# Scan products in pairs of runs, projections in a written order, and a new order of the first products, in a hybrid encoder layer

## The chip, the cores and the metric

The kernel runs on one core of one Trainium2 chip. Its metric is the device time of one execution in microseconds (us). Of an execution with the profiler there is a trace as well; its span runs from the first to the last instruction of the core.

## The reference

One layer works on 288 tokens: 256 of a new stream (prompt) and 32 of a running one (sample). Everything is float32.

```
xn   = rmsnorm(x);  proj = xn @ w_in          -> u (1024), z (2048), xBC (2560), dt (32)
pool = (mean over the last 2/4/8/16 tokens of u, minus u) @ w_pool, scaled
xs, B, C = silu(causal conv of 4 over xBC);   dt = softplus(dt + bias)
y    = exact chunked scan of xs with dt, B, C and a state h0, plus D * xs       (32 heads of 64)
ssd  = grouped rmsnorm(y * silu(z))
x    = x + rmsnorm(concat[pool, ssd] @ w_out)
x    = x + rmsnorm((silu(gate) * value) @ w_down),  gate, value = conv of 3 over rmsnorm(x) @ w_up
```

The outputs are x for both groups of tokens and the new histories and states. `w_in` is 2048 x 5664, `w_out` 3072 x 2048, `w_up` 2048 x 11264, `w_down` 5632 x 2048.

## The kernel before, in words

**Products.** Channels lie on the 128 partitions and the 288 tokens along the free axis. A float32 factor is split into a high and a low part (fp32r), and a product of two tiles is three matmuls of 128x128 by 128x288 (`mm3`, L150 to L156): high weight by high activation, high by low, low by high. All three go to one PSUM accumulator. Where a part of a group is *turned* (`TURNED`, counted by group and part), the last two change places.

**Groups.** `project` makes one or more blocks of 256 output columns. It fetches weights on SP's queue (`fetch_w`), splits them with ACT (high part, L146) and DVE (low part, L147) in parts of 4 input tiles by 256 columns, four buffers each, and issues 24 matmuls a part. A group on `w_in` has four parts, 96 matmuls. In the order of the program, groups 1 to 8 make xs, 9 to 16 make z, 17 to 19 make u, 20 to 25 use `w_out`, and from 26 on `w_up` and `w_down` follow. Tiles of PSUM: five for accumulators, three ("aux") for the rest.

**The first products.** Before group 1, B, C, the last two tiles of u, and dt are made from `w_first` in 11 chunks of 1, later 2, input tiles (`CHUNKS`; matmuls L379, those of dt L386). Six blocks of 128 columns come from each chunk. Chunk 0 arrives as three pieces: blocks 2 and 3, blocks 4 and 5, blocks 0 and 1. High and low weights of a chunk lie in one tile `w`, `W_GAP` floats apart. Twelve matmuls on ones (L284, tile `busy`) run before the first data are there. These products are issued in a written order.

**The scan.** The 32 heads are taken in eight runs of four (`ssd_quad`, q = 0 to 7), two 128-channel tiles of xs each. A run needs g broadcast to all partitions (`gb`, L597, POOL's queue), xs with tokens on partitions (`xk`, L611, POOL's queue), and then:

- xk times its weights on DVE (L628)
- the mask m, 128 x 4 x 416: twelve ACT operations (L633), one exponential on ACT (L636), one product on DVE (L638); m has two buffers
- 16 matmuls of 64 output channels, eight for each of the two tiles, two at a time on the two halves of the array's columns: k = 0, 1 the prompt (L651, L653), k = 2, 3 the sample (L655, L657). Each is two instructions in the trace; a run has 32
- two additions to xs on DVE, straight from PSUM

`XS_RATE` and `Z_RATE` say after which group of xs or z a run stands in the program. Gating with z, squares and their sums follow; two sums over channels (`psum_t`, L710) stand at the end of the sixth z group and of group 17.

**What sets the order on TensorE.** A scheduler orders each engine's instructions at build time by a modelled timeline: an instruction goes when its inputs are ready in the model, the earliest of the program first. `tc.issue_after(ins)` puts what it encloses behind `ins` on the same engine; `tc.keep_in_program_order(ins)`, called `pin`, puts an instruction behind the one that the program wrote last on its engine. Products in `project` are not pinned before; all but the first of a run's products are.

**w_out.** Groups 20 to 25 take input tiles 8 to 15, 16 to 23 (both ssd), then 0 to 7 (pool). Group 20 has two blocks of 256 columns, groups 21 to 24 one, group 25 two. Pool groups 1 and 0 (12 matmuls each, `pool_group`) are written into group 20, ahead of the splits of tiles 16 to 23.

## Time and profile before

| What | Before |
|---|---|
| median of 3 runs, us | 1308.37 |
| the runs, us | 1307.97 to 1308.87 |
| the profiled execution's own time, us | 1308.33 |
| its span, us | 1306.6 |
| TensorE instructions | 10043 |
| DVE, share of the span | 68% |
| ACT, share of the span | 51% |
| granted TensorE clock, mean | 0.999 |

The profiled execution's time is 1.7 us above its span; what the span shows is what the kernel's order decides. Starts and durations in rows are in us from the span's start. A row of the timeline gives start, duration from the first start to the last end, engine, line, operation, tiles, shapes, and count; in brackets stands the engine's idle time before it and what ended it. A row of the chain gives start, time, engine and tile, line, and count: there, time over count is the distance from one matmul's start to the next one's, which is the rate of TensorE. A matmul's own duration (294 ns for 128x288) overlaps its neighbours' and is no rate.

### The profile page before, as it was taken

To read this page: it belongs to the slowest core of one execution; us is meant where nothing else is said; L and a number is where in the kernel's file an instruction comes from. 1 tells how busy PE (TensorE), PEld (TensorE's weight loads), DVE (VectorE), ACT (ScalarE), POOL (GpSimd) and SP (SyncE) were. 2 spreads that over 40 slices of the span, in tenths; PEclk is the share of its full clock that TensorE was granted. 3 is DMA by queue.
4 is the path that set the end of the run, shared out by engine and by line. 5 is a ranking of instruction groups with operands and counts; after the bars stand their busy time and mean duration, and the time that the engine had idled before them with its cause. 6 is when DMAs were issued, how large, how long until landed. Compare 5 with 4: busy or idle time off the path is not lost.

```text
span 1306.6 us, 25261 instructions
## 1 busy us (share of the span) xinstructions
PE 1299.5 (99%) x10043; PEld 1289.3 (99%) x10043; DVE 894.7 (68%) x1515; ACT 672.8 (51%) x1013; POOL 244.8 (19%) x399
## 2 busy tenths in 40 slices
PE   9999999999999999999999999999999999999998
PEld 9999999999999999999999999999999999999997
DVE  7999988879645588977766643345666666754454
ACT  7557767446544566544444433334444444444442
POOL 2342212222222221211211100001111111201110
PEclk9999999999999999999999999999999999999999
DMA  9568875445666468766554445455544554466653
GB/s 345 187 212 278 292 218 182 162 153 201 213 218 212 154 198 259 214 186 190 174 171 162 157 174 171 158 180 174 182 162 162 175 174 169 162 233 188 212 180 115
DMA packets 110038, 251.75 MB, mean 193 GB/s; under 512 B 64736, under 2 KB 73856, under 8 KB 87392
## 3 DMA queue, kind: packets, MB, share of 16 engines
q1 hardware_dynamic: 103568, 233.36, 54.7%
q0 software_dynamic: 5824, 16.13, 4.1%
q8 instruction: 78, 1.28, 0.4%
q10 hardware_dynamic: 528, 0.66, 0.2%
q14 instruction: 40, 0.33, 0.1%
HBM read 237.11 MB, written 13.00 MB: 191 GB/s over the span
## 4 chain that ended last, share of the span: by engine, by line
PE 98%; DVE 0%; DMA 0%; ACT 0%; ACTq 0%; issue 0%
PE acc L156 91%; PE acc L379 2%; PE acc_x L156 1%; PE acc_x L379 1%; PE py L651 1%; PE acc L1283 0%; PE acc L1284 0%; PE py L653 0%; DMA raw<-in_w_first 0%; PE acc_t L1306 0%; PE pst L992 0%; PE acc L386 0%; DVE rm L1046 0%; PE py L657 0%; PE py L655 0%
## 5 line engine op out<-in xcount | busy, mean ns | idle before, releaser
L147 DVE TENSOR_TENSOR wlo<-raw,whi 128x1024 fp32r<-128x1024 f32 (+1 forms) x396 | 473.0, 1196 | 303.3 <-ACT whi L146 302.3
L146 ACT ACTIVATE whi<-raw 128x1024 fp32r<-128x1024 f32 (+1 forms) x396 | 408.2, 1032 | 466.6 <-PE acc L156 375.6
L156 PE MATMUL acc<-hn,whi 128*128 128x288 f32 x2752 | 538.6, 294 | 0.4 <-ACT hn L1059 0.4
L156 PEld LDWEIGHTS acc<-hn,whi 128*128 128x128 f32 x2752 | 436.4, 188 | 1.0 <-ACT hn L1059 0.9
L156 PE MATMUL acc<-hn,wlo 128*128 128x288 f32 x1376 | 399.7, 291 | 0.0
L156 PEld LDWEIGHTS acc<-hn,wlo 128*128 128x128 f32 x1376 | 258.9, 188 | 0.0
L156 PE MATMUL acc<-fa,whi 128*128 128x288 f32 x1320 | 257.5, 293 | 0.0
L156 PE MATMUL acc<-xn,whi 128*128 128x288 f32 x1216 | 239.1, 294 | 0.0
L156 PEld LDWEIGHTS acc<-fa,whi 128*128 128x128 f32 x1320 | 208.9, 188 | 0.0
L156 PEld LDWEIGHTS acc<-xn,whi 128*128 128x128 f32 x1216 | 193.1, 188 | 0.7 <-issue 0.5
L156 PE MATMUL acc<-fa,wlo 128*128 128x288 f32 x660 | 192.1, 291 | 0.0
L156 PE MATMUL acc<-xn,wlo 128*128 128x288 f32 x608 | 177.6, 293 | 0.0
L156 PEld LDWEIGHTS acc<-fa,wlo 128*128 128x128 f32 x660 | 124.3, 188 | 0.0
L1109 POOL COPY fc_stage<-ebuf 128x4 f32<-128x4 f32 x88 | 26.4, 299 | 471.6 <-DVE ebuf L1108 450.7
L156 PEld LDWEIGHTS acc<-xn,wlo 128*128 128x128 f32 x608 | 114.4, 188 | 0.1
L156 PE MATMUL acc<-mixs,whi 128*128 128x288 f32 x512 | 100.5, 294 | 0.0
L1115 DVE SCALAR_TENSOR_TENSOR fc<-ebuf,cols,fc 128x290 f32<-128x290 f32 x176 | 90.4, 517 | 3.9 <-ACT fc L1113 1.1
L1113 ACT ACTIVATE fc<-ebuf,cols 128x290 f32<-128x290 f32 x88 | 54.4, 623 | 73.2 <-DVE ebuf L1108 71.1
L1104 POOL COPY ebuf<-cols 128x2 f32<-128x2 f32 x88 | 69.9, 794 | 108.4 <-DVE fc L1115 96.0
L156 PEld LDWEIGHTS acc<-mixs,whi 128*128 128x128 f32 x512 | 81.3, 188 | 0.0
L156 PE MATMUL acc<-mixs,wlo 128*128 128x288 f32 x256 | 74.1, 293 | 0.0
L156 PE MATMUL acc<-mixp,whi 128*128 128x288 f32 x256 | 50.2, 293 | 0.0
(322 smaller groups left out, 1241.0 us busy)
## 6 DMA issues: line engine op xcount, KB each, us to landing
raw<-in_w_up SPq DMA_DIRECT2D x80, 1024.0 KB, 5.1
raw<-in_w_in SPq DMA_DIRECT2D x38, 1024.0 KB, 5.2
raw<-in_w_down SPq DMA_DIRECT2D x32, 1024.0 KB, 4.9
raw<-in_w_out SPq DMA_DIRECT2D x24, 1024.0 KB, 5.1
raw<-in_w_down SPq DMA_DIRECT2D x16, 768.0 KB, 4.2
raw<-in_w_up SPq DMA_DIRECT2D x14, 512.0 KB, 4.4
gb<-g_d POOLq DMA_DIRECT2D x8, 832.0 KB, 5.8
raw<-in_w_first SPq DMA_DIRECT2D x5, 768.0 KB, 12.3
```

What stands on the lines that cost most here:

```text
L146: act.activation(hi, raw[:, k : k + n, :], AF.Copy)
L147: dve.tensor_tensor(lo, raw[:, k : k + n, :], hi.bitcast(F32), op=ALU.subtract)
L156: pe.matmul(out, w, a[:, x, :], start=start and n == 0, stop=stop and n == 2)
L379: pin(pe.matmul(first[m], w[r][:, k, m * P : (m + 1) * P], xn[kb + k][:, x, :], start=kb + k + r + x == 0, stop=kb + k == KD - 1 and r == 1,))
L651: ins = pe.matmul(y[c, 0:256], xw[:, 0, f_], m[:, h, 0:256], start=True, stop=False)
L1104: pool.tensor_copy(e[:, 258:260], hist_f[:, :, i])
L1109: pool.tensor_copy(fc_stage[:, :, :, i], e[:, 256:324].rearrange("p (s c) -> p s c", c=34)[:, :, 0:2])
L1113: act.activation(c, e[:, 0:290], AF.Identity, bias=col["f_b"][:, i : i + 1], scale=f_w[:, 0, i : i + 1])
L1115: dve.scalar_tensor_tensor(c, e[:, r_ : r_ + 290], f_w[:, r_, i : i + 1], c, op0=ALU.mult, op1=ALU.add)
```

## The change

Four edits go together.

- **Runs in pairs.** `ssd_quad` is cut into the masks (`ssd_masks`) and the products (`ssd_products`). Masks are made for one run after a group as before (XS 2, 4, 7 and z 0, 2, 3, 4, 5); the products of two runs stand together after XS group 7 and z groups 1, 4 and 6, numbered from 0, so at the end of groups 8, 10, 13 and 15. A run's twelve ACT operations are queued behind the exponential of the run before. The prompt columns of a run's two tiles share one PSUM tile, and the sample columns of the pair share another, so an addition to xs becomes two (256 and 32 columns).
- **Program order.** From group 6 to 19 every product is pinned. In groups 20 and 21 the low weight comes first, and the other two of the three matmuls are pinned behind it. The list of turned parts is another, and can name several parts of a group.
- **First products.** In chunk 0, blocks 2 and 3 get all three of their matmuls first, then blocks 4 and 5, then 0 and 1. Chunks 4 and 5 take low-weight products second. High and low weights lie 48 floats apart instead of 16; `sq2` is 16 floats longer; `busy` takes the buffer of `sq`, and `ones_r`, made earlier, replaces it in the sums of squares.
- **Pool products later.** Pool groups 1 and 0 are written between the two column blocks of tiles 16 to 23 in group 20, whose last eight tiles are taken as 4 to 7, then 0 to 3.

```diff
@@ -37,8 +37,10 @@
 MW = 416
 EVAC = 100
 SUMS_AFTER = 2
-XS_RATE = (0, 0, 1, 0, 1, 0, 1, 0)
-Z_RATE = (1, 0, 1, 1, 0, 1, 1, 0)
+XS_RATE = (0, 0, 1, 0, 1, 0, 0, 1)
+Z_RATE = (1, 0, 1, 1, 1, 1, 0, 0)
+PAIR_XS = (7,)
+PAIR_Z = (1, 4, 6)
 TAIL = NT - P
 NB = 768
 CHUNKS = ((0, 1), (1, 1), (2, 1), (3, 1), (4, 1), (5, 1), (6, 2), (8, 2), (10, 2), (12, 2), (14, 2))
@@ -53,10 +55,14 @@
 TURN_AT = 13
 FC_GAP = 48
 NEAR = 8
-W_GAP = 16
-W_ROOM = 32
+W_GAP = 48
+W_ROOM = 64
+TURNED_FIRST = (4, 5)
+WHOLE = (20, 21)
+FIRST_WHOLE = 6
 TURNED = {
-    1: 0, 5: 3, 7: 2, 8: 1, 10: 1, 12: 1, 13: 1, 15: 1, 16: 1, 18: 1, 20: 8, 22: 0, 27: 0, 28: 1, 46: 0, 65: 0,
+    1: (0,), 5: (3,), 9: (0,), 11: (0,), 14: (0,), 15: (0,), 16: (0,), 18: (0,), 20: (0,), 22: (0,), 27: (0,),
+    28: (1,), 46: (0,), 65: (0,),
 }
 
 
@@ -148,16 +154,22 @@
             out.append([(kb + k + i, hi[:, i, :], lo[:, i, :]) for i in range(n)])
         return out
 
+    whole = [False]
+
     def mm3(out, wh, wl, a, start, stop, other=False):
         pairs = [(wh, 0), (wh, 1), (wl, 0)]
+        if whole[0] == 2:
+            pairs = pairs[2:] + pairs[:2]
         if other:
             pairs[1:] = pairs[:0:-1]
         for n, (w, x) in enumerate(pairs):
-            pe.matmul(out, w, a[:, x, :], start=start and n == 0, stop=stop and n == 2)
+            ins = pe.matmul(out, w, a[:, x, :], start=start and n == 0, stop=stop and n == 2)
+            if whole[0] and (n or whole[0] == 1):
+                pin(ins)
 
     groups_done = [0]
 
-    def project(view, groups, acts, ksplit, before=None, done=None, spare=(), hold=(), behind=None, wait=(), tail=()):
+    def project(view, groups, acts, ksplit, before=None, done=None, spare=(), hold=(), behind=None, wait=(), tail=(), middle=None):
 
 
         n_all = sum(-(-w // P) for _, w in groups)
@@ -165,7 +177,8 @@
         accs.extend(spare)
         k_first, k_last = ksplit[0][0], ksplit[-1][0] + ksplit[-1][1] - 1
         groups_done[0] += 1
-        turned = TURNED.get(groups_done[0])
+        turned = TURNED.get(groups_done[0], ())
+        whole[0] = (FIRST_WHOLE <= groups_done[0] <= WHOLE[1]) + (groups_done[0] in WHOLE)
         n_part = 0
         after = before(*ksplit[0]) if before else None
         for i, (kb, n) in enumerate(ksplit):
@@ -174,7 +187,9 @@
             if before and i + 1 < len(ksplit):
                 nxt = before(*ksplit[i + 1])
             m0 = 0
-            for raw, (c0, w) in zip(raws, groups):
+            for r, (raw, (c0, w)) in enumerate(zip(raws, groups)):
+                if middle and (i, r) == (1, 1):
+                    middle()
                 parts = split_w(raw, kb, n, w, tuple(wait) + ((after or ()) if m0 else ()) + (hold if i else tail if m0 + w // P == n_all else ()))
                 for q, part in enumerate(parts):
                     for m in range(w // P):
@@ -183,7 +198,7 @@
                             if behind and part[-1][0] == k_last and m0 + m > SUMS_AFTER:
                                 order.enter_context(tc.issue_after(behind[-1].ins))
                             for k, hi, lo in part:
-                                mm3(accs[m0 + m], hi[:, c], lo[:, c], acts[k], k == k_first, k == k_last, n_part == turned)
+                                mm3(accs[m0 + m], hi[:, c], lo[:, c], acts[k], k == k_first, k == k_last, n_part in turned)
                         if done and i + 1 == len(ksplit) and q + 1 == len(parts):
                             done(m0 + m, accs[m0 + m])
                     n_part += 1
@@ -206,7 +221,7 @@
     up_ = upool.enter_context(tc.tile_pool(name="upool", bufs=1))
     start = ExitStack()
     xin = start.enter_context(tc.tile_pool(name="xin", bufs=1))
-    busy = xin.tile([P, 2 * P], F32R, name="busy")
+    busy = xin.tile([P, 2 * NT], F32R, tag="sq", bufs=1, name="busy")[:, : 2 * P]
     pin(dve.memset(busy.bitcast(F32), 1.0))
     win = w_in
     O_Z, O_X = D_POOL, D_POOL + D_SSD
@@ -252,6 +267,7 @@
 
     ones = const.tile([P, P], F32, name="ones")
     pool.memset(ones, 1.0)
+    ones_r = const.tile([P, P], F32R, name="ones_r")
     eps_t = side1.tile([P, 1], F32, name="eps_t")
     pool.memset(eps_t, EPS)
     warm = const.tile([P, 1], F32, name="warm")
@@ -284,7 +300,7 @@
         pin(pe.matmul(first[1][:, : 2 * P], busy[:, 0:P], busy, start=True, stop=True))
     last_split = []
     lows = []
-    sq2 = xin.tile([P, 2 * NT], F32, name="sq2")
+    sq2 = xin.tile([P, 2 * NT + 16], F32, name="sq2")[:, : 2 * NT]
 
     def prepare(i):
 
@@ -348,6 +364,7 @@
                 squares(q)
         if i == 5:
             first_load(10)
+            pin(act.activation(ones_r, ones, AF.Copy))
             pin(dve.memset(ebuf[0][:, 0:1], 0.0))
             for e in ebuf + ubuf:
                 pin(pool.memset(e, 0.0))
@@ -362,15 +379,16 @@
             pin(dve.tensor_tensor(sq_r[:, NT:], sq2[:, :NT], sq_r[:, :NT].bitcast(F32), op=ALU.subtract))
         w = ahead_w.pop(0)
         products = [
-            (r, m, k, x) for m in (2, 3, 4, 5, 0, 1) for k in range(n) for r, x in ((0, 0), (0, 1), (1, 0))
+            (r, m, k, x) for m in (2, 3, 4, 5, 0, 1) for k in range(n)
+            for r, x in (((0, 0), (1, 0), (0, 1)) if i in TURNED_FIRST else ((0, 0), (0, 1), (1, 0)))
         ]
         if i == 0:
-            products.sort(key=lambda q: (q[1] < 2, q[0], q[3]))
+            products.sort(key=lambda q: ((q[1] + 4) % 6 // 2, q[0], q[3]))
         for q, (r, m, k, x) in enumerate(products):
             if i == len(CHUNKS) - 2 and q == 24:
                 p_ = aux([P, NT], "prs")
                 for c in (slice(0, NT), slice(NT, 2 * NT)):
-                    pin(pe.matmul(p_, busy[:, 0:P], sq_r[:, c], start=c.start == 0, stop=c.start > 0))
+                    pin(pe.matmul(p_, ones_r, sq_r[:, c], start=c.start == 0, stop=c.start > 0))
                 rstd = const.tile([P, NT], F32, tag="spread", bufs=3, name="rstd")
                 last_split[:] = [
                     pin(act.activation(rstd, p_, AF.Sqrt, bias=eps_t, scale=1.0 / D_MODEL)),
@@ -406,8 +424,6 @@
         dve.tensor_reduce(sel, id32.rearrange("h (t r) -> h r t", r=2), axis=AX.X, op=ALU.add)
         dve.tensor_reduce(pick, id32.rearrange("h (t r) -> h t r", r=2), axis=AX.X, op=ALU.add)
         dve.tensor_copy(sel64, sel.unsqueeze(2).broadcast_to([HEADS, 2, 64]))
-    ones_r = const.tile([P, P], F32R, name="ones_r")
-    pin(act.activation(ones_r, ones, AF.Copy))
     sc_stage = const.tile([P, 2, 3, NXC], F32, name="sc_stage")
     np_stage = const.tile([P, 2, 15, NU], F32, name="np_stage")
     hist_c = col["hist_c"].rearrange("p (r t) -> p r t", t=NXC)
@@ -605,6 +621,7 @@
 
     tokens = {}
     masked = []
+    exps = []
 
     def ssd_tokens(q):
         xk = mp.tile([P, 3, 2 * P], F32, tag="xk", bufs=3, name="xk")
@@ -612,7 +629,7 @@
         pool.dma_start(out=xk[:, 2, :], in_=xs_d[q][TAIL:, :])
         tokens[q] = xk
 
-    def ssd_quad(q):
+    def ssd_masks(q):
 
 
         gi = q // 4
@@ -630,18 +647,28 @@
         for j in range(4):
             for b, (lo_, hi_) in enumerate(((0, 256), (256, 384), (384, MW))):
                 h = 4 * q + j
-                act.activation(
-                    m[:, j, lo_:hi_], gb[:, j, lo_:hi_], AF.Relu, bias=tok[:, b, 0, h : h + 1], scale=-1.0
-                )
-        act.activation(m, m, AF.Exp, scale=-1.0)
+                with ExitStack() as order:
+                    if exps:
+                        order.enter_context(tc.issue_after(exps[-1].ins))
+                    act.activation(
+                        m[:, j, lo_:hi_], gb[:, j, lo_:hi_], AF.Relu, bias=tok[:, b, 0, h : h + 1], scale=-1.0
+                    )
+        exps.append(act.activation(m, m, AF.Exp, scale=-1.0))
         masked.append(
             dve.tensor_tensor(m, m, cbt[:, gi : gi + 1, :].broadcast_to([P, 4, MW]), op=ALU.mult)
         )
 
+        if q % 2 == 0:
+            ssd_first(q + 1)
+        return xw, m, h0t, ce
+
+    def ssd_products(q, sample, xw, m, h0t, ce):
+
+        rows_ = aux([P, 2 * NP_], "py")
         ys = []
         for i in range(2):
-            y = aux([P, NT], "py")
-            ys.append(y)
+            y, y_s = rows_[:, NP_ * i : NP_ * (i + 1)], sample[:, NS * (2 * (q % 2) + i) :][:, :NS]
+            ys.append((y, y_s))
             for k in range(4):
                 for j in range(2):
                     h = 2 * i + j
@@ -652,16 +679,19 @@
                     elif k == 1:
                         ins = pe.matmul(y[c, 128:256], xw[:, 1, f_], m[:, h, 256:384], start=False, stop=True)
                     elif k == 2:
-                        ins = pe.matmul(y[c, 256:], xw[:, 2, f_], m[:, h, 384:], start=True, stop=False)
+                        ins = pe.matmul(y_s[c, :], xw[:, 2, f_], m[:, h, 384:], start=True, stop=False)
                     else:
-                        ins = pe.matmul(y[c, 256:], h0t[:, i, c], ce[:, h, :], start=False, stop=True)
-                    if i or k or j:
-                        tc.keep_in_program_order(ins)
-        if q + 1 < NX // 2:
-            ssd_first(q + 1)
+                        ins = pe.matmul(y_s[c, :], h0t[:, i, c], ce[:, h, :], start=False, stop=True)
+                    pin(ins)
+        return ys
+
+    def ssd_add(q, ys):
+
         for i in range(2):
             t = 2 * q + i
-            dve.scalar_tensor_tensor(xs[t], xs[t], dcol[:, t : t + 1], ys[i], op0=ALU.mult, op1=ALU.add)
+            for c, y in zip((slice(0, NP_), slice(NP_, NT)), ys[i]):
+                o = xs[t][:, c]
+                dve.scalar_tensor_tensor(o, o, dcol[:, t : t + 1], y, op0=ALU.mult, op1=ALU.add)
 
     def token_sums(p_, sq, first_, last_, pin=False):
 
@@ -765,11 +795,22 @@
     done = [-1]
     rg = []
 
-    def run_quads(n):
+    masks_ = {}
+
+    def run_masks(n):
         for _ in range(n):
-            if quads and 2 * quads[0] + 1 < len(xs):
-                done[0] = 2 * quads[0] + 1
-                ssd_quad(quads.pop(0))
+            q = quads.pop(0)
+            masks_[q] = ssd_masks(q)
+
+    def run_pair():
+        sample = aux([P, 4 * NS], "py_s")
+        ys = {q: ssd_products(q, sample, *masks_[q]) for q in sorted(masks_)}
+        if quads:
+            ssd_first(quads[0])
+        for q in ys:
+            ssd_add(q, ys[q])
+            masks_.pop(q)
+            done[0] = 2 * q + 1
 
     def run_gates():
         while gates and gates[0] in zs and gates[0] <= done[0]:
@@ -781,7 +822,9 @@
         ps = project(win, [(O_X + 256 * i, 256)], xn, K16)
         xs_evac(i, ps)
         xs_conv(i - 1)
-        run_quads(XS_RATE[i])
+        if i in PAIR_XS:
+            run_pair()
+        run_masks(XS_RATE[i])
     for i in range(NX // 2):
         if Z_RATE[i]:
             ssd_tokens(quads[0])
@@ -792,7 +835,9 @@
             xs_conv(NX // 2 - 1)
         if i == 5:
             rg.append(rstd_all(gsum[0], 0.25 / 1024, "rg0", sq_parts(mp)))
-        run_quads(Z_RATE[i])
+        if i in PAIR_Z:
+            run_pair()
+        run_masks(Z_RATE[i])
         for j in range(2):
             gate_silu(2 * i + j)
         run_gates()
@@ -800,7 +845,6 @@
         if i > 5:
             for t in range(4 * i - 24, 4 * i - 20):
                 dve.tensor_tensor(xs[t], xs[t], rg[0], op=ALU.mult)
-    run_quads(NX)
     run_gates()
     for i in (NU - 2, NU - 1):
         rows_ = mp.tile([P, 4, MW], F32, tag="m", bufs=2, name="win_m")
@@ -809,7 +853,7 @@
             dve.scalar_tensor_tensor(
                 u[:, c], cur[:, c], 1.0 / WINDOWS[i // 2], u[:, c], op0=ALU.mult, op1=ALU.subtract
             )
-    assert not gates and not quads
+    assert not gates and not quads and not masks_
 
 
     ups = [project(win, [(512, 256)], xn, K16)]
@@ -1014,17 +1058,14 @@
     state_ops = {}
     last_ops = []
 
-    def mix_before(g):
-        def hook(kb, n):
-            if g == 0 and kb == 0:
-                pool_group(1)
-                pool_group(0)
-        return hook
+    def first_groups():
+        pool_group(1)
+        pool_group(0)
 
     for grp in ((0, 1), (2,), (3,), (4,), (5,), (6, 7)):
         project(
-            w_out, [(256 * c, 256) for c in grp], mix, [(8, 8), (16, 8), (0, 8)],
-            mix_before(grp[0]), lambda m, p_: mix_out(p_),
+            w_out, [(256 * c, 256) for c in grp], mix, [(8, 8), (16, 8), (4, 4), (0, 4)] if not grp[0] else [(8, 8), (16, 8), (0, 8)],
+            done=lambda m, p_: mix_out(p_), middle=None if grp[0] else first_groups,
         )
         if 2 <= grp[0] < 6:
             history(grp[0] - 2)
```

## The prediction

> **What bounds the kernel now.** First the page: the busy shares and the chain that ended last.
>
> ```profile
> span 1306.6 us, 25261 instructions
> ...
> PE 1299.5 (99%) x10043; PEld 1289.3 (99%) x10043; DVE 894.7 (68%) x1515; ACT 672.8 (51%) x1013; POOL 244.8 (19%) x399
> ...
> PE 98%; DVE 0%; DMA 0%; ACT 0%; ACTq 0%; issue 0%
> ```
>
> TensorE is busy through the span and carries the chain. So I asked for the waits next: TensorE's own, and the longest of ACT's on its products.
>
> ```profile
> PE acc_x L284 <- DVE busy L210: 1.3, 1, 1.3
> PE py__15339 L1348 <- ACT diag L1347: 1.0, 1, 1.0
> PE acc L156 <- ACT hn L1059: 0.4, 1, 0.4
> ```
> ```profile
> ACT whi L146 <- PE acc L156: 375.6, 222, 2.8
> ```
>
> TensorE waits three times, 2.7 us in all, nowhere in the mixer; ACT's splits wait for TensorE to free weight buffers, not the other way. No transfer and no other engine can give anything here. What can change is how far apart TensorE's matmuls start, which the chain in order of time shows as time over count.
>
> ```profile
> 21.71 3.15 PE acc L379 x24
> ...
> 108.97 17.21 PE acc L156 x131
> ...
> 128.06 5.56 PE acc L156 x40
> ...
> 135.51 7.30 PE acc L156 x54
> ...
> 144.70 25.04 PE acc L156 x190
> ...
> 171.64 25.23 PE acc L156 x192
> ...
> 280.93 13.40 PE acc L156 x102
> ...
> 309.15 6.95 PE acc L156 x52
> ...
> 316.36 6.68 PE acc L156 x50
> ...
> 331.00 38.20 PE acc L156 x292
> ...
> 515.92 763.10 PE acc L156 x5868
> ```
>
> The last row is the undisturbed rate: 763.10 / 5868 = 0.13004 us. Every other row is to be held against its count times 0.13004; what is over is all there is to win: 0.26 in the 192 after 171.64 (24.97 would do), 0.36 in the 40 after 128.06. The excess stands behind interruptions and dies out later. One interruption, in the timeline of TensorE:
>
> ```profile
> 196.58 0.29 PE L156 MATMUL acc<-xn,wlo 128*128 128x288 f32 x1
> 196.80 0.65 PE L651 MATMUL py<-m,xk 128*64 128x256 f32 x4
> ...
> 197.59 0.29 PE L657 MATMUL py<-ce,h0t 128*64 128x32 f32 x4
> 197.70 0.63 PE L651 MATMUL py<-m,xk 128*64 128x256 f32 x4
> ...
> 198.47 0.29 PE L657 MATMUL py<-ce,h0t 128*64 128x32 f32 x4
> 198.69 0.53 PE L156 MATMUL acc<-xn,whi 128*128 128x288 f32 x2
> 199.06 0.30 PE L156 MATMUL acc<-xn,wlo 128*128 128x288 f32 x1
> ```
>
> Going in, the last product takes 0.22 instead of 0.13 (0.09 more). Coming out, the last four of L657 take 0.22, where the same four between the run's two tiles take 0.11 (0.11 more), and the first two products 0.37 instead of 0.26 (0.11 more): 0.31 us at the borders. From the row after 171.64, 0.26 less 0.20 for its own first two products and the next way in leaves 0.06 that dies out behind. So **an interruption costs 0.37 us**, and passing from one tile of a run to the next costs none of it.
>
> **The change, part by part.**
>
> *Runs in pairs.* The 256 instructions of the scan stay; four of eight interruptions go: 4 x 0.37 = 1.48. The three early runs stand among products in broken order: their rows have 0.36, 0.28 and 0.33 over, against 0.26 in a regular one, 0.19 together; the program order takes this back, I count 0.15. The sum at the end of group 14 stands in front of a run now, inside its interruption; in the changed kernel no run follows there. The row after the other such sum (102 products after 280.93) is 0.14 over; I charge 0.10. Net **1.53**; bounds 1.2 (nothing for order, 0.14 for the sum, 0.05 more behind each pair) and 1.9 (no charge, the 0.06 of each remaining pair gone too).
>
> An addition to xs becomes two: 16 more of 32 columns on DVE, at the 0.18 us of L445 below, four a pair. TensorE doesn't wait for them, and the gates that do have a group's time; without that cover a pair would hold DVE up by 0.7 us. The masks in turn put a mask's ACT operations behind the exponential of the one before (L636, 1.58 us, below); only the next mask is queued behind it, which a pair needs last anyway. The moved `ones_r` is one short ACT operation, with ACT at 51%.
>
> *Program order, groups 6 to 19.* Its cost is a stall wherever a pinned product's factor is late: behind it stand all later products, and behind them the splits that wait for buffers. For weights the row of ACT's waits is the cover: the buffers are full. I take 0, and treat the masks as a rival.
>
> *w_out, low weight first, pool groups later.* The rows after 309.15, 316.36 and 331.00 are 0.19, 0.18 and 0.23 over; 0.6 in all. There the scheduler mixes products of pool groups and of several accumulators. With the low weight in front, which DVE finishes last, the other two of the three are ready when it is, so the three stay together. Bounds 0 (the mixing stays) and 0.6; nearest is the even rate of the long row, so I take **0.55**. The pool groups are the same 24 matmuls. Their two fetches now go to SP's queue behind one more of w_out's, and the last eight tiles come in twice as many fetches of half the size, which hold two more of the four raw buffers. One whole fetch lands in 5.1 us:
>
> ```profile
> raw<-in_w_out SPq DMA_DIRECT2D x24, 1024.0 KB, 5.1
> ```
>
> It is wanted 48 products, 6.2 us, after the one before at the earliest, so I cost it at nothing; were the cover gone, TensorE would wait up to 5.1 once.
>
> *First products.* The start, in the timeline, and then the chain:
>
> ```profile
> 4.24 0.52 DVE L305 SCALAR_TENSOR_TENSOR xn<-xg,xn 128x288 fp32r<-128x288 f32 x1
> 4.28 0.50 PEld L379 LDWEIGHTS acc<-xn,w 128*128 128x128 f32 x2 [0.38 <-ACT xn L302]
> ...
> 4.67 0.94 DVE L328 TENSOR_TENSOR w<-raw,w 128x256 fp32r<-128x256 f32 x2
> 4.74 0.89 ACT L323 ACTIVATE w<-raw 128x256 fp32r<-128x256 f32 x2 [0.54 <-DMA raw<-in_w_first]
> ...
> 5.21 0.29 PEld L379 LDWEIGHTS acc<-xn,w 128*128 128x128 f32 x1 [0.43 <-ACT w L323]
> ```
> ```profile
> 7.98 1.44 PE acc_x L379 x6
> 9.42 2.06 PE acc L379 x12
> 11.48 0.79 PE acc_x L379 x6
> ```
>
> Two products of blocks 2 and 3 start, then TensorE waits 0.43 us for the second piece's high part. After the change their products with the low activation come next, which DVE has at 4.76 (4.24 + 0.52), and then those with the low weight, at 5.1 (4.67 and half of 0.94). So the wait, and the slow start after it, are filled with two products. They run at the early rate, 1.44 / 6 = 0.24; the last row has 0.79 / 6 = 0.13, and the 12 between, in 2.06, are some 4 at the one and 8 at the other, so the rate changes near 10.4. Two products more that stand ahead of that change save 2 x 0.13. **0.25**; bounds 0 and 0.45 (two at 0.24).
>
> The gap between high and low weights: the 24 products after 21.71 take 3.15, 0.1312 each, 0.0012 over the undisturbed rate; for some 270 of them 0.33. No row shows what a gap does. Bounds -0.33 and +0.33; I take **0.20**, nearer to the rate of L156, whose two parts lie in separate tiles.
>
> Sum: 1.53 + 0.55 + 0.25 + 0.20 = 2.53. The profiled execution's 1308.33 (span 1306.6 and 1.7 around it), which is within 0.04 of the median, becomes **1305.8 us**.
>
> **The rivals.**
>
> *The early rate ends one step earlier.* The twelve matmuls on ones don't end it, nor the broken stretch up to 5.21; some 5 us of dense work do. With the wait gone the dense work begins at 4.3. If the change of rate comes earlier by that, 0.9 us, some 4 products gain 0.11 each, 0.4; if nearly all of the 20 that run at 0.24 after 5.21 are spared it, 2.2. Between the two, 12 x 0.11 = 1.3 more: **1304.5**. For it: the idle time ahead of 5.21 shrinks. Against it: nothing in the trace says how dense is enough. The Trainium skill, "TensorE: Matmul & The Clock Gate", Part 1, says that the array runs at half clock until a free-running window of about 3.4 us was busy enough. By that rule the change comes either one whole window earlier, an estimate of 3.4 / 0.24 = 14 products and 1.5 us, or not at all. The trace agrees with the halving (0.24 against 0.13); that windows decide, no row here shows.
>
> *The order gains little.* The mixing in w_out stays or the new turned parts set off as much excess as they end, the gap does nothing: 1.2 + 0.25 + 0.2 = 1.7, so **1306.7**. For it: the 0.06 to 0.14 behind every break, which no row shows going away by an order.
>
> *A pair comes up before its masks: slower.* m has two buffers, so both masks of a pair are made after the pair before, in turn. Between the pairs after groups 8 and 10, and 13 and 15, stand two groups, 25.2 us by the row after 171.64. One mask's length, from the timelines of ACT and DVE, and how full both were where masks and xs convolutions meet:
>
> ```profile
> 171.57 1.02 ACT L633 ACTIVATE m<-gb,tok 128x256 f32<-128x256 f32 x3 [0.33 <-PE py L655]
> ...
> 176.69 1.58 ACT L636 ACTIVATE m<-m 128x1664 f32<-128x1664 f32 x1
> ```
> ```profile
> 180.81 1.89 DVE L638 TENSOR_TENSOR m<-m,cbt 128x1664 f32<-128x1664 f32 x1
> ...
> 182.94 0.18 DVE L445 SCALAR_TENSOR_TENSOR xs<-tanh,conv 128x32 f32<-128x32 f32 x1
> ```
> ```profile
> 140.00:150.00 10.00, 10.00 (x94) 9.51 (x93) 10.00 (x19) 10.00 (x23) 3.30 (x5) 1.00 0.74 238
> 150.00:160.00 10.00, 10.00 (x79) 10.00 (x78) 9.59 (x16) 5.09 (x6) 2.34 (x4) 1.00 0.95 324
> ```
>
> From 171.57 to 182.70 it takes 11.1 us, two of them 22.3: it fits by 2.9. DVE (third figure after the stretch) and ACT (fourth) are full in one stretch of these, and the second mask stands behind a convolution and splits. If two masks need over 25.2 us, TensorE stands still for the rest; at 15 us a mask that is 4.8 us at group 10, and, were it so at group 15 as well, 9.6. With the one: 1305.8 + 4.8 = **1310.6**, with both 1315. It decides against the change from 2.5 us in all: from 13.9 us a mask if one pair waits, from 13.2 if both do. Against it: the stretch after 150 has ACT half idle (5.09), and nothing but m's buffers keeps a mask's work from beginning ahead of its place in the program.
>
> **How the numbers follow.** Forecast 0.46, with 1305.0 (all upper bounds: 1.9 + 0.6 + 0.45 + 0.33) to 1306.6 (two lower bounds at once); the earlier rate 0.28, with 1303.5 (2.2) to 1305.4 (0.4); little from the order 0.17, with 1306.4 to 1307.4; the late mask 0.09, from 1306.5 on. A measurement of this kernel can tell about 0.2% (2.6 us) from no change, so faster means under 1305.75, slower over 1311. Faster: all of the second case and a bit over half of the first, 0.28 + 0.24 = 0.52. Slower: 0.05 of the late mask, and 0.02 for other stalls of pinned products. Same: the rest, 0.41. The range 1303.5 to 1307.5 leaves out most of the late mask and little else.
>
> **What would show it.** Right: L651 in four stretches of TensorE instead of eight, each followed by a row some 0.2 to 0.3 over its count; no wait of TensorE on m, xk or splits among its waits; rows of w_out after 309 at 0.130 to 0.131; ten products of chunk 0 begun by 6.7 without the wait on L323. Wrong: a TensorE wait of over 0.5 us at L651 with DVE's L638 as what ended it; rows at 0.133 or more in groups 6 to 21; the rate of L379 unchanged at 0.131 refutes the gap's 0.20, and a change of rate near 7 instead of 10.4 makes the first rival true.

## The result, and the profile after

The changed kernel takes 1305.49 us (median of 14 runs, 1304.22 to 1306.34) against 1308.40 us for the kernel before beside it (14 runs, 1307.69 to 1308.98): a ratio of 0.9977, interval 0.9969 to 0.9984. The forecast was 1305.8. The profiled execution was the longest of the 14, 1306.34 us, 1.99 less than that of before. Line numbers have moved: the products are now L166, the first products L397, the scan's products L678 to L684, the sums over channels L740.

The page: span, busy shares, and the chain that ended last.

```profile
span 1304.6 us, 25289 instructions
...
PE 1296.9 (99%) x10043; PEld 1286.6 (99%) x10043; DVE 897.0 (69%) x1531; ACT 671.6 (51%) x1013; POOL 251.7 (19%) x399
...
PE 96%; DMA 1%; DVE 1%; ACT 1%; issue 0%; SPq 0%; ACTq 0%
```

TensorE is 2.6 us less busy with the same 10043 matmuls, and the chain has left it for 4% of the span, against 2% before. Its waits say where:

```profile
PE acc_x L300 <- DVE busy L225: 1.3, 1, 1.3
PE py__15355 L1389 <- ACT diag L1388: 0.7, 1, 0.7
PE acc L166 <- ACT hn L1100: 0.4, 1, 0.4
PE acc L397 <- ACT xn L318: 0.3, 1, 0.3
PE acc L397 <- DVE w L334: 0.3, 1, 0.3
```

Two are new, both in the first products (L397). None is on m, xk or the weights of a group. The chain in order of time, mixer and w_out:

```profile
108.88 41.64 PE acc L166 x319
150.52 0.58 PE py L678 x4
...
154.18 25.22 PE acc L166 x192
179.39 0.58 PE py L678 x4
...
183.05 37.70 PE acc L166 x288
220.75 0.58 PE py L678 x4
...
224.40 12.74 PE acc L166 x96
...
237.41 12.55 PE acc L166 x96
249.97 0.58 PE py L678 x4
...
253.62 25.22 PE acc L166 x192
278.85 0.27 PE psum_t L740 x2
...
307.27 19.56 PE acc L166 x150
...
328.40 38.22 PE acc L166 x294
```

The scan stands in four stretches instead of eight. The row behind each is 0.25 or 0.26 us over its count times 0.13004, as after a single run before: a pair of runs costs one interruption. From the first product after `pcb` to the second `psum_t` the profiles have 171.69 us before and 169.97 after, so the mixer gives **1.72**; from there to the end of the small matmuls `pst`, behind group 21, they have 90.17 and 89.39, so w_out gives **0.78** (150 products in 19.56 is 0.1304 each). These stages are taken from the starts themselves, so a row's rounding can differ by 0.01. In the chain the row of group 1 starts at 47.56 instead of 47.66: **0.10**. The first group of up, from its first product to the sum over channels (`psum_t`) behind it, takes 38.98 instead of 38.45, a **loss of 0.53**. 1.72 + 0.78 + 0.10 - 0.53 = 2.07, for spans that differ by 2.02. The medians differ by 2.91; on the rest see the end of the account below.

### The profile page after: what moved, and what is told of

Read it like the earlier page. It is cut to its first block, busy times and chain, and to the rows that moved or that the text cites. A ratio compares the mean times of both kernels' runs of the same rounds, so it can differ in the third digit from the quotient of the medians.

```text
span 1304.6 us, 25289 instructions
## 1 busy us (share of the span) xinstructions
PE 1296.9 (99%) x10043; PEld 1286.6 (99%) x10043; DVE 897.0 (69%) x1531; ACT 671.6 (51%) x1013; POOL 251.7 (19%) x399
## 4 chain that ended last, share of the span: by engine, by line
PE 96%; DMA 1%; DVE 1%; ACT 1%; issue 0%; SPq 0%; ACTq 0%
PE acc L166 91%; PE acc_x L166 1%; DMA raw<-in_w_first 1%; PE py L678 1%; PE acc L1324 0%; DVE w L334 0%; PE acc L1325 0%; DMA xg<-in_x_g 0%; PE acc_t L1347 0%; DVE sq L354 0%; PE py L680 0%; PE acc_x L397 0%; PE acc L397 0%; DVE xn L321 0%; PE pst L1036 0%
## 5 line engine op out<-in xcount | busy, mean ns | idle before, releaser
L166 PE MATMUL acc<-hn,whi 128*128 128x288 f32 x2752 | 539.0, 294 | 0.5 <-ACT hn L1100 0.4
L166 PEld LDWEIGHTS acc<-hn,whi 128*128 128x128 f32 x2752 | 436.3, 188 | 1.5 <-ACT hn L1100 0.8
L166 PE MATMUL acc<-hn,wlo 128*128 128x288 f32 x1376 | 399.6, 291 | 0.0
L166 PEld LDWEIGHTS acc<-hn,wlo 128*128 128x128 f32 x1376 | 259.0, 188 | 0.0
L166 PE MATMUL acc<-fa,whi 128*128 128x288 f32 x1320 | 257.5, 293 | 0.0
L166 PE MATMUL acc<-xn,whi 128*128 128x288 f32 x1216 | 238.5, 294 | 0.0
L166 PEld LDWEIGHTS acc<-fa,whi 128*128 128x128 f32 x1320 | 208.9, 188 | 0.0
L166 PEld LDWEIGHTS acc<-xn,whi 128*128 128x128 f32 x1216 | 192.9, 188 | 0.6 <-issue 0.5
L166 PE MATMUL acc<-fa,wlo 128*128 128x288 f32 x660 | 192.1, 291 | 0.0
L166 PE MATMUL acc<-xn,wlo 128*128 128x288 f32 x608 | 177.4, 292 | 0.0
L166 PEld LDWEIGHTS acc<-fa,wlo 128*128 128x128 f32 x660 | 124.3, 188 | 0.0
L166 PEld LDWEIGHTS acc<-xn,wlo 128*128 128x128 f32 x608 | 114.5, 188 | 0.0
L166 PE MATMUL acc<-mixs,whi 128*128 128x288 f32 x512 | 100.2, 293 | 0.0
L166 PEld LDWEIGHTS acc<-mixs,whi 128*128 128x128 f32 x512 | 81.1, 188 | 0.0
L166 PE MATMUL acc<-mixs,wlo 128*128 128x288 f32 x256 | 74.6, 291 | 0.0
L166 PE MATMUL acc<-mixp,whi 128*128 128x288 f32 x256 | 50.1, 293 | 0.0
```

What stands on the lines that cost most here:

```text
L166: ins = pe.matmul(out, w, a[:, x, :], start=start and n == 0, stop=stop and n == 2)
```

## The experiments

Every time is a median beside the kernel before (1308.37 to 1308.41 in these comparisons); stage times are from the profiles, one execution each. The kernel before itself varies by 1.3 to 2.7 us from run to run in one comparison, and no interval is narrower than 0.15%, so terms of some tenths of a microsecond are read from the stages. Two of the stages repeat well: the mixer takes 169.97 in all seven profiles that have its order unchanged, and w_out 89.39 in nine. The stage of the first products does not: group 1 starts between 46.51 and 47.56 in the five profiles that have the changed kernel's code up to there.

**The scan's runs one by one**, in the program's order, with turned first parts behind the added breaks too.

```diff
-PAIR_XS = (7,)
-PAIR_Z = (1, 4, 6)
+PAIR_XS = (6, 7)
+PAIR_Z = (0, 1, 3, 4, 5, 6)
...
```

> The changed kernel with the runs of the scan one by one again, each behind a group and in program order, with the part behind each turned. Theory S: four more interruptions of 0.37 us, less 0.10 since the sum stands in front of a run again: 1.3 to 1.5 us over the changed kernel, so 1.4 to 1.6 under the kernel before; from the first product after group 5's small matmuls to the sum behind group 17 1.4 more than the changed kernel's 169.97 us (108.88 to 278.85). Rival O (the program order alone carries the mixer's gain, pairs nothing): within 0.3 us of the changed kernel there.

1306.60, 0.9986 [0.9977, 0.9995]; mixer 171.11. The kernel had seven interruptions, not eight: both masks of the first two runs were ready after xs group 6, and the chain shows them together at 137.38. Three more than the changed kernel's four cost 171.11 - 169.97 = 1.14, so **0.38 each**; the forecast had 0.37. The price isn't pure: behind each of the three stands one more turned part, which costs 0.05 by the run without them below, and one sum over channels stands inside an interruption again, which saves 0.07. Without both it is some 0.35, an estimate: (1.14 - 0.15 + 0.07) / 3. Four times 0.38 is 1.52 of the 1.72.

**Pairs without the program order** in groups 6 to 19.

```diff
-whole[0] = (FIRST_WHOLE <= groups_done[0] <= WHOLE[1]) + (groups_done[0] in WHOLE)
+whole[0] = 2 * (groups_done[0] in WHOLE)
```

> The changed kernel with no product of groups 6 to 19 pinned; pairs and w_out stay. Theory S: the order is worth what the early rows had over the regular ones, 0.15 to 0.2 us; the stretch 108.88 to 278.85 grows by 0.1 to 0.4. Rival O: it grows by 1 us or more.

1306.66, 0.9986 [0.9977, 0.9994]; mixer 171.18, so 1.21 of the 1.72 are gone, far more than my theory gave the order. Its chain:

```profile
107.82 42.00 PE acc L166 x319
...
153.48 25.67 PE acc L166 x194
...
182.81 38.09 PE acc L166 x286
```

The same stretch of 286 products takes 0.1332 each here and 0.1309 in the changed kernel (37.70 over 288). It is no excess that dies out: from 195 us on, every six products repeat the same starts, 133 ns apart in the mean, to the next pair; 0.65 of the 1.21 lie in this stretch. So there are **two steady rates**, 0.130 and 0.133, and this stretch, once in the slower, stays there. In the trace's list of starts both have the same cycle of two products by high weights and one by a low weight; the slower begins where the scheduler has put products out of this cycle. That is one way into it and not the only one, as runs below show. Pairs are worth 1.5 by the run above, and the order 0.2 on single runs: 171.69 - 171.11 = 0.58, of which 0.38 are the one interruption fewer. The two are not additive: here the pairs kept 0.51 of their gain without a written order (171.69 - 171.18).

**The first products undone** in the changed kernel, and **they alone** in the kernel before; then **the gap alone undone**, and **the order of chunk 0 alone undone**.

```diff
-W_GAP = 48
+W_GAP = 16
...
-TURNED_FIRST = (4, 5)
+TURNED_FIRST = ()
...
-products.sort(key=lambda q: ((q[1] + 4) % 6 // 2, q[0], q[3]))
+products.sort(key=lambda q: (q[1] < 2, q[0], q[3]))
```

> The changed kernel with the first products as before (order of chunk 0, gap 16, no turned chunks, busy in its own tile); pairs, program order and w_out as changed. Theory S (TensorE's spacing in the mixer carries the gain, the first products almost none): 2.3 to 2.8 us under the kernel before, and group 1 begins within 0.3 us of 47.66. Rival F (the first products carry it, by an earlier end of the early rate): 1.5 us or less under it.

> The kernel before with the edits of the first products alone. Theory S: within 0.5 us of the kernel before; the products of the chunks start 0.130 us apart, but the wait on DVE's low weights (some 0.5 us near 30 us) and on the sums of squares (some 0.5 us near 38 us) take back what an early change of rate gives, so group 1 begins at 47.2 to 47.7. Rival F: 1.3 us or more under the kernel before, group 1 begins under 46.5.

> The changed kernel with the gap of 16 floats between high and low weights again (and sq2 16 floats shorter). If the gap sets the rate of the first products, they start 0.1311 us apart again instead of 0.1300, 0.3 us over their 288; the time hardly moves (under 0.3 us), as the chunks are late anyway. If it doesn't, 0.1300 stays, and the rate came from the turned order.

> The changed kernel with the products of chunk 0 in the order of before. Theory: TensorE waits 0.4 us for the second piece again; two products fewer stand ahead of the change of rate. The time moves by -0.2 to +0.4 us, since the chunks near 30 and 38 us are late whenever the early rate ends early. Rival F: 1 us or more over the changed kernel.

1305.56 without them, 0.9978 [0.997, 0.9987]; alone 1308.19, 1.0002 [0.9993, 1.0011]; without the gap 1305.36, 0.9978 [0.9968, 0.9987]; with the old order 1305.86, 0.9982 [0.9973, 0.9991]. The four edits together are worth 0.07 us in the one pairing and 0.19 in the other: nothing that shows, though intervals of some 1.2 us either way don't exclude the forecast 0.45. TensorE does begin more products. It is twelve instead of ten between 6 and 8 us and fifteen instead of ten between 8 and 10; the third and fourth columns are TensorE's busy time and count.

```profile
6.00:8.00 2.00, 2.00 (x12) 2.00 (x11) 1.00 1.00 352
8.00:10.00 2.00, 2.00 (x15) 1.79 (x14) 1.00 1.01 376
```
```profile
6.00:8.00 2.00, 2.00 (x10) 2.00 (x9) 1.00 1.04 363
8.00:10.00 2.00, 2.00 (x10) 2.00 (x10) 1.00 1.01 373
```

(Changed kernel above, before below.) This is not the order's work alone, since the rate changes at 7.4 us in the one and at 10.4 in the other. With all four edits undone, and the change at 6.7, it is fourteen and seventeen. The order shows before the change: up to 6 us seven products have begun in the kernel with w_out undone (new order, first one at 4.35) and five in that of before (first one at 4.31), the two of the forecast. Where it went is in the chain of the changed kernel, which before runs over TensorE alone from 5.21 to 47.66:

```profile
8.53 13.05 DMA raw<-in_w_first
...
21.66 1.50 ACT w L330
...
23.18 1.76 DVE w L334
...
28.60 1.46 DVE w L334
...
38.84 0.40 PE prs L391
...
45.49 2.08 PE acc L404 x32
```

The stage is now set by a piece of `w_first` that lands at 21.58, then by VectorE making low weights and squares. The products of dt start 45.49 - 21.58 = 23.91 us after the landing; with the first products alone:

```profile
8.07 12.34 DMA raw<-in_w_first
...
44.32 2.08 PE acc L389 x32
```

44.32 - 20.41 = 23.91 again. TensorE runs earlier, into weights that aren't made. In the ten profiles whose chain takes this way, with these steps in their places, the distance is 23.89 to 24.07, while the landing itself lies between 20.37 and 21.58; the changed kernel's is the latest.

The gap does not do what it was costed for. With 16 floats, 24 products of the last chunk take 3.15 in all three profiles; the chain of the kernel without the gap, which has already passed VectorE there:

```profile
37.72 0.47 DVE sq_r L379
...
38.23 0.40 PE prs L391
...
40.21 3.15 PE acc L397 x24
```

With 48 floats they take 3.12 in five profiles and 3.19 or 3.20 in six. The changed kernel, and then the kernel without the turned first parts (below), which has the same first products in the same order:

```profile
40.81 3.12 PE acc L397 x24
```
```profile
40.01 3.20 PE acc L397 x24
```

So the wider gap takes these products from 0.1312 to one of the two rates, 0.1300 or 0.1333, and the same written order falls into either; what decides is not shown. With the old order of chunk 0, where TensorE carries the chain to the end, the products of dt start at 45.66, and at 45.58 before: the gap and the turned chunks give nothing there.

Even the kernel with all four edits undone has the chain through VectorE (L334, L354) in its profile, where the rate changed at 6.7 us. The profile of before, with its change at 10.4, showed an execution in which TensorE was last.

**VectorE's work moved**: the product of `w_dt` behind the sums of squares, and the two matmuls of these sums 12 products later, at the start of the last chunk. Then the same **with the products of group 1 in the program's order** (the diff's last pair), and **the product of `w_dt` alone moved**.

```diff
-        if i == 6:
-            pin(dve.tensor_tensor(
-                w_dt, w_dt, g_mix_pre.unsqueeze(2).broadcast_to([P, KD, HEADS]), op=ALU.mult
-            ))
...
-            if i == len(CHUNKS) - 2 and q == 24:
+            if i == len(CHUNKS) - 1 and q == 0:
...
-whole[0] = (FIRST_WHOLE <= groups_done[0] <= WHOLE[1]) + (groups_done[0] in WHOLE)
+whole[0] = (groups_done[0] == 1 or FIRST_WHOLE <= groups_done[0] <= WHOLE[1]) + (groups_done[0] in WHOLE)
```

> The changed kernel with two pieces of DVE's and TensorE's work in the first products moved: the product of w_dt with the norm's weights stands behind the sums of squares instead of ahead of chunk 7's low weights, and the sums' two matmuls stand at the start of the last chunk, 12 products later. Theory (what an early end of the early rate gives is lost to late low weights and late squares): both waits near 30 and 38 us go or shrink to under 0.15 us each; where the rate changes near 7 us, group 1 begins near 46.7, 0.8 us earlier, and the median is 0.3 to 0.9 us under the changed kernel's. Rival (the transfers of w_first bound it): the waits move to the next chunk, and the time stays within 0.2.

1308.07, 0.9998 [0.9989, 1.0007], 2.6 us over the changed kernel. The stage itself did gain:

```profile
7.31 13.84 DMA raw<-in_w_first
...
44.51 2.08 PE acc L403 x32
```

44.51 - 21.15 = 23.36 after the landing, 0.55 less than 23.91: the moved work was in the way. The row of group 1 starts at 46.59, 0.97 earlier; the other 0.4 is a landing that came earlier in this execution. The loss is behind that. The scheduler had written group 1 in another order.

```profile
46.59 62.29 PE acc L166 x466
```

0.1337 each against 0.1306 for the 449 before `pcb` in the changed kernel: the slower rate, for 60 us.

> The kernel with the sums of squares a chunk later and the product of w_dt behind them, which had cost 2.6 us, now with the products of group 1 in the program's order as well. Theory (the loss came from TensorE alone: a displaced order of products in group 1 left a slower steady pattern, 133.3 instead of 130.0 ns a product, from 48 us to 109 us and again from 126 to 150): the slower pattern is gone, 2 to 2.6 us come back, 1305.0-1305.8, or 1304.7 if the earlier start of group 1 is kept. Rival (VectorE was late with what the groups wait for): 1307.5-1308.1, with the waits for VectorE in the list of TensorE's waits.

1306.55, 0.9988 [0.9979, 0.9997].

```profile
46.58 60.86 PE acc L166 x466
...
110.12 23.67 PE acc L166 x181
133.82 0.51 DVE conv L454
...
172.17 1.14 DVE wlo L153
173.35 6.40 PE acc L166 x46
```

The same 466 products take 1.43 us less, and the median falls by 1.52: the written order cures that stretch, as the theory of the rate has it. The remaining 1.06 over the changed kernel point to the rival: the chain leaves TensorE from 133.8 to 173.3 us for convolutions and low weights on VectorE, and TensorE waits for it:

```profile
PE acc L166 <- DVE wlo L153: 0.5, 1, 0.5
```

The wait is not all of it. Behind it, and before that behind one product that starts 0.06 late near 134 us, the products run at 0.1333 to the next pair, in the usual cycle of weights. So a short delay can start the slower rate as well, without a product out of order. Both causes were at work. And in this profile, with VectorE's work moved, the chain of the first products runs over TensorE alone again, up to 46.58 instead of 47.66 before.

> The changed kernel, with the product of w_dt and the gains on VectorE moved from the step of chunk 6 to behind the last sums of squares; every TensorE instruction stays in its place. In the changed kernel the profile shows TensorE idle for 0.3 us at 29.9 for low weights and 0.5 us at 38 for the squares, both made by VectorE. Theory (the first products gain little because VectorE is late once they run faster): at least one of these stalls goes, group 1 starts 0.5 to 0.9 us earlier in the profile relative to the clock change, and the median falls from 1305.5 to 1304.7-1305.1. Rival (the first products end when their weights land, whatever VectorE does): no stall goes, 1305.4-1305.6.

1305.12, 0.9976 [0.9967, 0.9986]. The median is just above the theory's range, but the mechanism isn't there: no stall went.

```profile
7.72 13.28 DMA raw<-in_w_first
...
36.88 0.47 DVE sq L372
...
38.23 0.40 PE prs L390
...
45.02 2.08 PE acc L403 x32
```

45.02 - 21.00 = 24.02 after the landing, no better than 23.91. So the 0.55 above comes of the place of the sums, which gave VectorE 12 products more for the squares. The difference of 0.37 between the medians is within the intervals, and this doesn't explain it.

**w_out undone**: pool products early, whole fetches, no written order in groups 20 and 21, and the turned part of group 20 as before (the diff in parts).

```diff
-whole[0] = (FIRST_WHOLE <= groups_done[0] <= WHOLE[1]) + (groups_done[0] in WHOLE)
+whole[0] = FIRST_WHOLE <= groups_done[0] < WHOLE[0]
...
-            w_out, [(256 * c, 256) for c in grp], mix, [(8, 8), (16, 8), (4, 4), (0, 4)] if not grp[0] else [(8, 8), (16, 8), (0, 8)],
+            w_out, [(256 * c, 256) for c in grp], mix, [(8, 8), (16, 8), (0, 8)],
...
```

> The changed kernel with w_out as before: high weight first and nothing pinned in groups 20 and 21, pool groups 1 and 0 ahead of the splits of tiles 16 to 23, the last eight tiles in one fetch, the turned parts of before. Theory S: the 0.6 to 0.8 us that this stage gave come back: from the sum behind group 17 to the end of group 21's state products 0.6 to 0.8 more than the changed kernel's 89.4 us (278.85 to 368.23), and 2.0 to 2.4 us in all under the kernel before. Rival: the order of the earlier groups evens this stage out by itself; under 0.2 more.

1305.86, 0.9981 [0.9972, 0.999]; the stage takes 90.10 instead of 89.39, so 0.71 of the 0.78 is these edits, and the mixing is back in the chain, with 0.1337 for each of 52 products:

```profile
306.21 6.95 PE acc L166 x52
```

**The turned first parts out** of groups 9, 11, 14, 15, 16 and 18.

```diff
-    1: (0,), 5: (3,), 9: (0,), 11: (0,), 14: (0,), 15: (0,), 16: (0,), 18: (0,), 20: (0,),
+    1: (0,), 5: (3,), 20: (0,),
```

> The changed kernel without the turned first parts of groups 9, 11, 14, 15, 16 and 18: their products all stand in the usual order; interruptions, pairs and program order stay. Theory (after a break TensorE's products settle in one of two steady patterns, 130.0 or 133.3 ns, and the turned part decides which): some stretches between two breaks run wholly at 133, 3.3 ns a product more on up to 1000 products; the mixer's 169.97 us become 171.0-173.2, median 1306.5-1308.7. Rival (turning only shortens the 0.06 to 0.14 us of excess behind each break, as the prediction had it): 0.1-0.6 us more, 1305.6-1306.1, every stretch at 130.

1304.78, 0.9971 [0.9959, 0.9983], the lowest of all, of six runs. Theory and rival both fall: turning doesn't choose the rate in the mixer, and it shortens nothing.

```profile
153.49 25.17 PE acc L166 x192
...
182.31 37.65 PE acc L166 x288
...
223.61 12.69 PE acc L166 x96
```

Each row is 0.05 shorter than in the changed kernel, the mixer 0.28 (169.69). That the whole kernel is faster than the changed one by this is not resolved: the medians' 0.7 lies within the intervals.

**A ninth row of x early**, on top of the moved product of `w_dt`, for the loss in up.

```diff
-NEAR = 8
+NEAR = 9
```

The loss of up, in the list of waits of the changed kernel, against 3.8 us in three waits before:

```profile
ACT hn L1100 <- DMA mg<-in_x_g: 6.6, 2, 4.9
```

> As the kernel with the product of w_dt later, and in the up stage the ninth row of x is also loaded early and added on VectorE, so that seven rows instead of eight are added by DMAs on GpSimd's queue. Theory (the first of these DMAs lands too late for ScalarE, which then delays the up weights by 0.3 to 0.5 us): against the kernel without this, the first group of up takes 38.4-38.5 instead of 38.6-39.1 and the median is 0.2-0.5 us lower. Rival (the ninth addition of 0.45 us on VectorE and its row of x come in the way, or the next DMA is late in its place): nothing to 0.4 us more.

1305.76, 0.9979 [0.9971, 0.9988]. Against the kernel with the product of `w_dt` moved, the first group of up does fall, from 38.72 to 38.37, but w_out rises from 89.39 to 89.86 and what follows up to the up stage from 99.70 to 99.93. The sum goes the rival's way, but its reasons, a late addition or a late row, aren't what the trace shows. 294 products in w_out take 38.69 instead of 38.22:

```profile
327.82 38.69 PE acc L166 x294
```

From 341 to 359 us they run at 0.132 and then at 0.1333, with high and low weights in the same order as in the changed kernel. What set that off stays open.

## Why the prediction was right, point by point

- **Pairs and order, 1.53: 1.72 measured.** The price of an interruption was right (0.37; 0.38, or some 0.35 pure). The 0.20 left stands for the order's 0.15 and the sum's -0.10; behind the lone sum the row is 12.55 for 96, 0.07 over. The reason given for the order was too small: excess behind breaks that it takes back. It keeps stretches from the slower rate, in the kernel with pairs 0.65 of the 1.21 in one of them, while the turned parts cost 0.28.
- **Program order costs 0: right.** No wait on a split, mask or xk came up. Nor did a pair come up before its masks, so the slower rival fell.
- **w_out, 0.55: 0.78**, of which 0.71 go with the edits. The rows are at 0.1304 and 0.1300.
- **The first products, 0.45: 0.07 and 0.19 by the medians, which can't tell this from 0.45.** This is the step that failed, in its reasons. Both terms, the filled wait (0.25) and the gap (0.20), assumed that TensorE sets that stage's end; the prediction says that no transfer and no other engine can give anything. In the profile of before it was so; I didn't ask what is late next. In eleven of the fourteen profiles the chain goes through a landing of `w_first` and VectorE, and giving VectorE 12 products more for the squares shortened the way from that landing by 0.55. The filled wait is there, as two products; the gap's 0.20 isn't, since the wider gap gives 0.1300 or 0.1333. The sign of ten products begun by 6.7 us was missed by one: it is nine, the first of them at 4.50 instead of 4.31, without the wait on the second piece.
- **The early rate ends earlier: the mechanism came, its gain did not show.** The rate changes at 7.4 us in the changed kernel. That was the sign named for the rival at 1304.5; the median is 1.0 above that, and in the profile the landing takes the gain back. Why it comes when it does was read wrongly: in the kernel with the gap alone undone it changes at 4.28 us, before the first of these products at 4.43, so it takes no dense work after the matmuls on ones.
- **Not foreseen: up's first group**, 0.53 longer in the changed kernel's profile. Across the kernels with the new w_out it took 38.4 to 39.3 us; in before and the two kernels with the old one 38.44 and 38.45. But in the kernel without program order, which has the new w_out too, it is 38.44. It also differs between executions of the same code: from group 1 on the kernels with the first products undone, without the gap and with the old order of chunk 0 are the changed kernel, and take 38.72, 38.73 and 39.09. ScalarE waits there for rows of x that DMAs add up, but the length doesn't follow these waits (5.1 us of them for 38.44 without program order, 4.4 for 39.00 with single runs); the cause stays open.

That the total came within 0.3 us is in part luck. The forecast has 0.4 too little for mixer and w_out, perhaps 0.3 too much for the first products, and nothing for up. The stages of the two profiles add up to 2.07, and the medians differ by 2.91; where the other 0.84 are is not shown. They may lie in the first products' stage: the changed kernel's profile is of its longest run and has the latest landing of `w_first`, 21.58, where the four others with the same code up to group 1 have 20.37 to 20.91.

## What to carry to other kernels

Where a stage's chain lies on one engine, a faster engine is worth only the slack of what feeds it: before counting a gain, work out from the landing of the stage's data when the next engine would be done. An edit that touches other engines can rewrite the matmul order and lose more than it wins; where that order matters, write it down, and compare time over count in every stretch after each edit. Price a removed interruption from its borders, and check the price by putting some back. Before pricing a stage that starts on a transfer, look at several executions of the same code: here its end varied by 1 us.

## What the runs showed of the hardware

- Groups of three matmuls (two by the high weight, one by the low), each with its weight load, run for long at one of two steady rates in the same order of weights: a period of six of 126, 131, 130, 132, 131, 130 ns (0.1300 in the mean) or of 139, 133, 134, 133, 135, 126 ns (0.1333). Shorter stretches also show 0.1312 (first products with 16 floats between high and low weights), 0.132 and 0.1344. The slower began behind products out of the cycle (without program order), behind a product 0.06 late (group 1 pinned), and once with neither in sight (ninth row of x early); the same written order of the first products ran at either. What in the array or its memories makes the two was not tried.
- The trace's record of the granted clock has one stretch at full clock: 1293.651 us in the three kernels with the old order of chunk 0, 1297.065 in ten with the new one and 1300.478 in the eleventh. The steps are 3.414 and 3.413 us, and the lengths 379, 380 and 381 of them. That agrees with the Trainium skill, "TensorE: Matmul & The Clock Gate", Part 1, on a free-running window of about 3.4 us, which no row of before showed. The change comes between 4.3 and 7.4 us with the new order and at 6.7, 10.3 and 10.4 with the old one. Two of those three come some 3 us or more after all with the new order; the third doesn't, and its shorter stretch comes of an earlier end (1300.36 us from the start, against 1303.60 for the first products alone, which change at 6.5). So that the order wins a window is likely and not shown.
